# Forgetting attention: the two halves of a block's accumulator, added by GpSimd from a copy and a DMA move instead of by VectorE from PSUM

## The chip, the cores and the metric

The kernel runs on one core of a Trainium2 chip. The metric is the device time of one execution in microseconds (us): 2538.94 us is the median of three runs before the change (2537.07 to 2539.52).

A core has TensorE for matrix products (PE, with PEld for its weight loads), VectorE (DVE), ScalarE (ACT), GpSimd (POOL) and SyncE (SP), which here issues nearly all DMA transfers. PE writes to PSUM, an accumulation memory of banks; the other working memory is SBUF with 128 partitions (rows).

## What is computed

Two layers of an encoder block on 2048 tokens of width 1024, all in float32. Per layer: RMS norm, one input projection, three token mixers, a SiLU gate on each, one output projection, RMS norm and residual. The change touches the third mixer, the forgetting attention with 6 heads of width 64:

```python
cum_f = jnp.cumsum(jax.nn.log_sigmoid(f_logit.astype(jnp.float32)), axis=1)
...
for i in range(s // Q_BLOCK):
    logits = jnp.einsum('bqhd,bkhd->bhqk', qb, kb).astype(jnp.float32) * scale
    logits = logits + cum_f[:, :, q0:q1, None] - cum_f[:, :, None, :q1]
    logits = jnp.where(causal, logits, -jnp.inf)
    p = jax.nn.softmax(logits, axis=-1).astype(v.dtype)
    outs.append(jnp.einsum('bhqk,bkhd->bqhd', p, vb))
...
f_out = f_out.reshape(b, s, F_WIDTH) * jax.nn.silu(f_g)
```

## The kernel before

A float32 product is made of products of a rounded high part and a remainder (H and L). For the attention the values V are stored as 128 columns, 64 of the high part and 64 of the remainder, so one matmul of V with the weights P gives a PSUM tile `acc` of 128 rows: rows 0 to 63 hold P times the high part, rows 64 to 127 P times the remainder. The attention output of a block is the sum of the two halves.

The attention stage of a layer (`fox`) goes over 6 heads h, 4 query blocks s of 512 tokens, and the 4s+4 key tiles j of 128 tokens that block s can see: 40 steps per head, 240 per layer. The instructions of every engine stand in the order in which the program writes them; each engine, and SP's list of DMAs, works its own list in that order and waits where a semaphore says so. A step writes, in this order:

- `l_step`: DVE makes the remainder PL of the last transposed tile (L672);
- `t_step`: PE transposes the softmax weights of a tile three steps ahead of their use (L661), ACT rounds them into PH (L673). For a few tiles (`ON_POOL`) ACT copies the transposed tile out of PSUM (L666) and GpSimd makes PH and PL (L667, L668);
- `e_step`: ACT takes exponentials (L648);
- `s_step`: PE makes scores well ahead (L614, L615), DVE masks them and takes the running minimum (L632);
- `v_step`: PE multiplies V with PH and PL into `acc` (L690, L691); after the last key tile of a block `finish` is added to the background;
- then SP issues one waiting load (`ld.issue()`, L569), and every background generator goes one step on (`bg.tick()`).

`finish` runs once per head and block, 24 times a layer. ACT copies the lower half of `acc` to SBUF (L703), DVE adds the upper half from PSUM into rows 0 to 63 or 64 to 127 of `o2`, by the head's parity e = h % 2 (L705), and sums the softmax denominators (L710). For an even head that is all. For an odd head, with both heads of a pair in `o2`, the reciprocals go through a transpose (L719, L721), a 4 KB DMA store `rd` to device memory (L723), and two DMA loads `gy<-rd` that spread them over the rows (L726); L726 waits until `rd` has landed. GpSimd multiplies them into the gate (L728) and the result into `o2` (L730), and SP stores the block (L732). FX, RA, RB, RC, RD are the steps left between these.

Loads of the next head: at the end of a head's first block, for h > 0, `ld.kv(h + 1)` queues three loads of K and V (512, 512 and 1024 KB, L569), which are issued one per step behind it. For h = 0 and 1 they are issued earlier, in the projection; after head 5 there is none. So they stand in SP's list behind `finish` of block 0 of heads 1 to 4. The tiles named U share 29 buffers.

Of the kernel before, what the change touches and what calls it, by code (L numbers as in the profile page):

```python
# [10 lines left out]
F32 = mybir.dt.float32  # L11
F32R = mybir.dt.float32r
AF = mybir.ActivationFunctionType
ALU = mybir.AluOpType
# [4 lines left out]
P = 128  # L19
# [4 lines left out]
HD = 64  # L24
# [13 lines left out]
FX, RA, RB, RC, RD = 2, 2, 4, 1, 3  # L38
# [32 lines left out]
def wait(n):  # L71
    for _ in range(n):
        yield
# [3 lines left out]
def trunk(ctx, tc, a, out):  # L77
    nc = tc.nc
# [8 lines left out]
    up = ctx.enter_context(tc.tile_pool(name="up", bufs=NU))  # L87
# [3 lines left out]
    def U(name, dt=F32):  # L91
        return up.tile([P, 1024], dt, name=name, tag="u")
# [3 lines left out]
    def bank(name, tag):  # L96
        n, bufs = BANKS[tag]
        return ps.tile([P, n], F32, name=name, tag=tag, bufs=bufs)
# [4 lines left out]
    def small(name, shape, bufs=4):  # L103
        return tp.tile(shape, F32, name=name, tag=name, bufs=bufs)
# [466 lines left out]
    class Fox:  # L571
# [124 lines left out]
        def finish(self, h, s, acc):  # L696
            m, e = divmod(h, 2)
            if e == 0 and s % 2 == 0:
                self.o2[s // 2] = U("o2")
            o2 = self.o2[s // 2][:, (s % 2) * 512:(s % 2 + 1) * 512]  # L700
            yield
            lo = up.tile([HD, 512], F32, name="lo", tag="u")
            nc.scalar.copy(out=lo, in_=acc[HD:P, :])  # L703
            yield
            nc.vector.tensor_tensor(out=o2[e * HD:(e + 1) * HD], in0=acc[0:HD, :], in1=lo, op=ALU.add)  # L705
            if e == 0:
                self.rd[s] = small("rd", [P, 2, 4], bufs=6)
            rd = self.rd[s]
            den = self.den.pop((h, s))
            nc.vector.tensor_reduce(out=rd[:, e], in_=den[:, :, 0:s // 2 + 1], op=ALU.add, axis=AX.X)  # L710
            if e == 0:
                return
            nc.vector.reciprocal(out=rd, in_=rd)
            gy = U("gy")
            g, rb = gy[:, 0:512], gy[:, 512:1024]
            nc.sync.dma_start(out=g, in_=self.gscr[m][:, s * 512:(s + 1) * 512])
            yield from wait(FX)
            T = bank("rT", "S")
            nc.tensor.transpose(T[0:8, 0:P], rd.rearrange("p e r -> p (e r)"), ident)  # L719
            rT = tp.tile([8, P], F32, name="rT", tag="yr")  # L720
            nc.scalar.activation(out=rT, in_=T[0:8, 0:P], func=AF.Copy, scale=0.5)  # L721
            scr = dram.tile([8, P], F32, name=f"rd{self.ld.l}{m}{s}")
            nc.sync.dma_start(out=scr, in_=rT)  # L723
            yield from wait(RA)
            for i in range(2):
                nc.sync.dma_start(out=rb[i * HD:(i + 1) * HD], in_=scr[4 * i:4 * i + 4].rearrange("r p -> (r p)").partition_broadcast(HD))  # L726
            yield from wait(RB)
            nc.gpsimd.tensor_tensor(out=g, in0=g, in1=rb, op=ALU.mult)  # L728
            yield from wait(RC)
            nc.gpsimd.tensor_tensor(out=rb, in0=o2, in1=g, op=ALU.mult)  # L730
            yield from wait(RD)
            nc.sync.dma_start(out=self.y[s][1][m], in_=rb)  # L732
# [204 lines left out]
    for l in range(depth):  # L937
# [3 lines left out]
        for i in fox(fx):  # L941
            if i >= len(fx.V) - OW and i % OD:
                next(og, None)
            if l == depth - 1 and i == len(fx.V) - OPRE:
                op = out_proj(l, y, W, og, x_src, lambda t: out[t * P:(t + 1) * P, :], None, None, None)
            elif i == len(fx.V) - OPRE:
# [5 lines left out]
                op = out_proj(l, y, W, og, x_src, lambda t, x1=x1: x1[t], hT, (nw, W0), cur)  # L952
# [44 lines left out]
```

## Time and profile before

| what | value |
| --- | --- |
| median of three runs | 2538.94 us |
| the profiled execution | 2536.31 us |
| its span in the trace | 2534.5 us |
| PE busy | 2490.1 us, 98% |
| PEld busy | 2141.2 us, 84% |
| DVE busy | 1660.3 us, 66% |
| ACT busy | 1258.1 us, 50% |
| POOL busy | 863.2 us, 34% |
| attention stages (first to last `acc` matmul) | about 795 to 1086 us and 2053 to 2344 us |

The sum in the prediction is made against the profiled execution's 2536.31 us, which lies 2.63 us below the median of the runs; 1.8 us of it lie outside the span. Engine times are sums over the whole span; what an engine does in one stage is read from a view of that stretch. A number in brackets behind a row of an engine is idle time just before it, with what ended it. A row of SPq is a DMA being issued by SP: its start is when SP had waited for everything the DMA waits for, not when the data move.

### The profile page before, as it was taken

How to read it: one execution, taken by the hardware profiler on the slowest of the kernel's cores; microseconds unless marked ns; L12 is line 12 of the kernel's file. 1: busy time of each engine (PE TensorE's matmuls, PEld its weight loads, DVE VectorE, ACT ScalarE, POOL GpSimd, SP SyncE). 2: the span in 40 equal slices, each digit the busy share in tenths (PEclk: the TensorE clock that was granted, in tenths of full speed). 3: DMA queues.
4: the chain of work that ended last, by engine and by line, in shares of the span. 5: the costliest groups of instructions: out<-in, count | busy, mean ns of one | idle time of the engine just before them, and what ended most of it. 6: DMA issues, size and time to landing. Idle time of an engine off the chain costs nothing.

```text
span 2534.5 us, 39560 instructions
## 1 busy us (share of the span) xinstructions
PE 2490.1 (98%) x13112; PEld 2141.2 (84%) x13112; DVE 1660.3 (66%) x4161; ACT 1258.1 (50%) x2967; POOL 863.2 (34%) x1384
## 2 busy tenths in 40 slices
PE   9999999999999999999999999999999999999998
PEld 8988899787888888878898889997878888887887
DVE  5544477666668999844454445776666789998433
ACT  7634434333335888843344444333333368888222
POOL 3111367444433334331120114664443333244200
PEclk9999999999999999999999999999999999999999
DMA  6435411101041345253432354111010414543443
GB/s 210 120 92 122 110 46 34 41 14 42 10 110 41 102 110 147 72 182 132 138 124 75 98 121 114 29 38 44 13 39 18 106 42 108 122 135 105 154 149 117
DMA packets 187061, 229.87 MB, mean 91 GB/s; under 512 B 23272, under 2 KB 128680, under 8 KB 185320
## 3 DMA queue, kind: packets, MB, share of 16 engines
q1 hardware_dynamic: 186712, 227.08, 32.0%
q8 instruction: 104, 1.70, 0.3%
q14 instruction: 101, 0.83, 0.1%
q10 hardware_dynamic: 144, 0.26, 0.0%
HBM read 149.20 MB, written 78.09 MB: 90 GB/s over the span
## 4 chain that ended last, share of the span: by engine, by line
PE 83%; DVE 9%; ACT 3%; POOL 2%; issue 2%; DMA 1%; SPq 0%; ACTq 0%; POOLq 0%; DVEq 0%
PE oo L870 13%; PE z L491 10%; PE z L493 10%; PE z L492 10%; PE T L661 6%; PE z L267 5%; PE z L266 5%; PE z L268 5%; PE S L614 4%; PE S L615 4%; PE acc L691 3%; PE acc L690 3%; DVE HL L178 3%; ACT HL L176 2%; PE sc L371 1%
## 5 line engine op out<-in xcount | busy, mean ns | idle before, releaser
L491 PE MATMUL z<-HL 128*128 128x512 f32 (+2 forms) x1536 | 589.4, 384 | 2.3 <-ACT HL L176 2.3
L493 PE MATMUL z<-HL 128*128 128x512 f32 (+2 forms) x1536 | 560.8, 365 | 1.2 <-DVE HL L178 1.0
L492 PE MATMUL z<-HL 128*128 128x512 f32 (+2 forms) x1536 | 559.4, 364 | 0.6 <-POOL HL L178 0.6
L178 DVE TENSOR_TENSOR HL<-hT,HL 128x512 fp32r<-128x512 f32 x576 | 425.3, 787 | 42.0 <-ACT HL L176 33.6
L870 PE MATMUL oo<-HL 128*128 128x512 f32 x1488 | 355.4, 395 | 0.1
L178 POOL TENSOR_TENSOR HL<-wf,HL 128x384 fp32r<-128x384 f32 (+2 forms) x162 | 190.1, 1179 | 431.4 <-ACT HL L176 277.5
L176 ACT CAST HL<-hT 128x512 fp32r<-128x512 f32 x576 | 323.6, 625 | 0.0
L870 PEld LDWEIGHTS oo<-HL 128*128 128x128 f32 x1488 | 273.3, 188 | 57.8 <-DVE HL L178 0.5
L493 PEld LDWEIGHTS z<-HL 128*128 128x128 f32 x1536 | 289.0, 188 | 36.1 <-DVE HL L178 2.6
L491 PEld LDWEIGHTS z<-HL 128*128 128x128 f32 x1536 | 289.7, 189 | 25.3 <-ACT HL L176 3.2
L492 PEld LDWEIGHTS z<-HL 128*128 128x128 f32 x1536 | 290.5, 189 | 22.8 <-POOL HL L178 0.9
L672 DVE TENSOR_TENSOR PHL<-T,PHL 128x512 fp32r<-128x512 f32 (+3 forms) x402 | 241.1, 603 | 16.3 <-ACT PHL L673 16.2
L673 ACT CAST PHL<-T 128x512 fp32r<-128x512 f32 (+3 forms) x402 | 206.2, 520 | 57.2 <-PE T L661 41.0
L266 PE MATMUL z<-HL 128*128 128x512 f32 x576 | 224.5, 390 | 0.0
L268 PE MATMUL z<-HL 128*128 128x512 f32 x576 | 224.1, 389 | 0.0
L267 PE MATMUL z<-HL 128*128 128x512 f32 x576 | 224.1, 389 | 0.0
L350 ACT COPY v<-z 128x128 f32<-128x128 f32 x96 | 25.5, 266 | 382.4 <-DVE w L346 382.3
L614 PE MATMUL S<-kv,q 128*128 128x512 f32 (+1 forms) x480 | 210.9, 441 | 3.0 <-DVE mn L632 3.0
L690 PE MATMUL acc<-PHL,kv 128*128 128x512 f32 x480 | 181.0, 377 | 0.0
L691 PE MATMUL acc<-PHL,kv 128*128 128x512 f32 x480 | 176.3, 367 | 1.3 <-POOL PHL L668 0.7
L648 ACT ACTIVATE row<-row,mn 128x1024 f32<-128x1024 f32 (+2 forms) x192 | 158.2, 824 | 35.5 <-DVE mn L632 35.5
L615 PE MATMUL S<-kL,q 66*128 66x512 f32 (+1 forms) x480 | 175.8, 366 | 0.0
(160 smaller groups left out, 4343.7 us busy)
## 6 DMA issues: line engine op xcount, KB each, us to landing
x<-x SPq DMA_DIRECT2D x48, 512.0 KB
qk<-zHL SPq DMA_DIRECT2D x192, 128.0 KB
wf<-w_in SPq DMA_DIRECT2D x96, 192.0 KB
vscr<-vv SPq DMA_DIRECT2D x32, 384.0 KB
wf<-w_in SPq DMA_DIRECT2D x48, 256.0 KB
kv<-qk SPq DMA_DIRECT2D x24, 512.0 KB
kv<-vscr SPq DMA_DIRECT2D x12, 1024.0 KB
q<-qk SPq DMA_DIRECT2D x48, 256.0 KB
```

What stands on the lines that cost most here:

```text
L176: nc.scalar.copy(out=v(H), in_=src)
L178: eng.tensor_tensor(out=v(L), in0=src, in1=v(H), op=ALU.subtract)
L266: mm(z, lhsT=wH[:, c], rhs=H, start=(k == 0), stop=False)
L267: mm(z, lhsT=wH[:, c], rhs=L, start=False, stop=False)
L268: mm(z, lhsT=wL[:, c], rhs=H, start=False, stop=(k == KT - 1))
L491: mm(z[:, :n], lhsT=H[:, c], rhs=wH[:, :n], start=(k == 0), stop=False)
L492: mm(z[:, :n], lhsT=H[:, c], rhs=wL[:, :n], start=False, stop=False)
L493: mm(z[:, :n], lhsT=L[:, c], rhs=wH[:, :n], start=False, stop=(k == KT - 1))
L614: mm(S[:, :n], lhsT=Q[0][:, qc], rhs=K[:, kc], start=True, stop=False)
L615: mm(S[:, :n], lhsT=Q[1][0:HD + 2, qc], rhs=self.ld.C[h][c // 2][0:HD + 2, (c % 2) * 512:(c % 2) * 512 + n], start=False, stop=True)
L690: mm(self.acc[:, c0:], lhsT=V[:, j], rhs=PH[:, c0:], start=(j == 0), stop=False)
L870: mm(oo[g], lhsT=x[:, c], rhs=w[g][i], start=(k == 0 and first), stop=(k == KT - 1 and last))
```

## The change

ACT now copies all 128 rows of `acc` into the left half of a 1024-wide tile `two`. A DMA on SP's list moves the other head half's 64 rows beside the 64 rows that belong to this head. GpSimd adds the two, 8 steps later for an even head and just ahead of the gate product for an odd one. DVE's add is gone. The line numbers of what follows move by 3 or 4: L719, L723, L726, L728, L730, L732 become L722, L726, L729, L732, L734, L736.

```diff
             yield
-            lo = up.tile([HD, 512], F32, name="lo", tag="u")
-            nc.scalar.copy(out=lo, in_=acc[HD:P, :])
+            two = U("two")
+            mine, other = (slice(e * HD, (e + 1) * HD), slice((1 - e) * HD, (2 - e) * HD))
+            nc.scalar.copy(out=two[:, 0:512], in_=acc)
+            nc.sync.dma_start(out=two[mine, 512:1024], in_=two[other, 0:512])
             yield
-            nc.vector.tensor_tensor(out=o2[e * HD:(e + 1) * HD], in0=acc[0:HD, :], in1=lo, op=ALU.add)
...
             if e == 0:
+                yield from wait(FX + RA + RB)
+                nc.gpsimd.tensor_tensor(out=o2[mine], in0=two[mine, 0:512], in1=two[mine, 512:1024], op=ALU.add)
                 return
...
             yield from wait(RB)
+            nc.gpsimd.tensor_tensor(out=o2[mine], in0=two[mine, 0:512], in1=two[mine, 512:1024], op=ALU.add)
             nc.gpsimd.tensor_tensor(out=g, in0=g, in1=rb, op=ALU.mult)
```

SP's list before, around block 0 of head 1 in layer 0: the last loads of queries, the three loads of head 2's K and V (`kv_9310`), the gate, then the store `rd` and the two loads that wait for it.

```order
L569 DMA q_9269<-qk001_238 128x512
L569 DMA q_9269<-qk001_238 66x512
L569 DMA kv_9310<-qk011_241 64x2048
L716 DMA gy_9326<-gscr00_244 128x512
L569 DMA kv_9310<-qk011_241 64x2048
L569 DMA kv_9310<-vscr0_243 128x16x128
L723 DMA rd000_9366<-rT_9364 8x128
L726 DMA gy_9326<-rd000_9366 64x512 x2
```

SP's list after, at the same place; `two_9243` is the move of head 0, block 3, and `two_9311` that of head 1, block 0.

```order
L705 DMA two_9243<-two_9243 64x512
L569 DMA q_9272<-qk001_238 128x512
L569 DMA q_9272<-qk001_238 66x512
L705 DMA two_9311<-two_9311 64x512
L569 DMA kv_9314<-qk011_241 64x2048
L719 DMA gy_9329<-gscr00_244 128x512
L569 DMA kv_9314<-qk011_241 64x2048
L569 DMA kv_9314<-vscr0_243 128x16x128
L726 DMA rd000_9369<-rT_9367 8x128
L729 DMA gy_9329<-rd000_9369 64x512 x2
```

Each move waits for ACT's copy of its block; what stands below it in SP's list now comes after that copy, the loads of K and V of the next head among it.

GpSimd's list before, from the tile of head 1, block 1 (128x384) to that of block 2, key tile 4 (`PHL_9476`):

```order
L667 TENSOR_SCALAR PHL_9349<-Ts_9350 128x384
L668 TENSOR_TENSOR PHL_9349<-Ts_9350,PHL_9349 128x384
L728 TENSOR_TENSOR gy_9326<-gy_9326 128x512
L667 TENSOR_SCALAR PHL_9476<-Ts_9477 128x512
L668 TENSOR_TENSOR PHL_9476<-Ts_9477,PHL_9476 128x512
L730 TENSOR_TENSOR gy_9326<-o2_8595,gy_9326 128x512
```

GpSimd's list after, at the same place; L714 adds head 0's block 3, L731 head 1's block 0:

```order
L667 TENSOR_SCALAR PHL_9352<-Ts_9353 128x384
L668 TENSOR_TENSOR PHL_9352<-Ts_9353,PHL_9352 128x384
L714 TENSOR_TENSOR o2_8968<-two_9243 64x512
L731 TENSOR_TENSOR o2_8595<-two_9311 64x512
L732 TENSOR_TENSOR gy_9329<-gy_9329 128x512
L667 TENSOR_SCALAR PHL_9481<-Ts_9482 128x512
L668 TENSOR_TENSOR PHL_9481<-Ts_9482,PHL_9481 128x512
L734 TENSOR_TENSOR gy_9329<-o2_8595,gy_9329 128x512
```

The two adds stand ahead of the gate product; the gate product stands ahead of the next tile for PE, as it did.

## Rows read from the trace of the kernel before

**Rows 1.** Attention stages: length, busy PE, PEld, DVE, ACT, POOL; clock, DMA share, GB/s.

```profile
795.00:1092.00 297.00, 290.61 (x1781) 245.15 (x1780) 266.23 (x723) 254.60 (x559) 110.91 (x119) 1.00 0.42 114
2052.00:2349.00 297.00, 290.26 (x1776) 244.79 (x1776) 267.17 (x724) 254.91 (x559) 110.48 (x119) 1.00 0.41 112
```

**Rows 2.** Waits of PE, whole span: total us, times, longest.

```profile
PE T L661 <- DVE PHL L672: 7.2, 15, 1.3
PE S L614 <- DVE mn L632: 3.0, 7, 0.9
PE acc L691 <- POOL PHL L668: 0.7, 1, 0.7
```

**Rows 3.** Groups by line and shape: xcount, busy us, mean ns, idle before.

```profile
L673 ACT CAST PHL<-T 128x512 fp32r<-128x512 f32 x282 | 162.2, 585 | 31.1 <-PE T L661 22.4 <-PE S L614 5.8 <-POOL w L348 0.7
L705 DVE TENSOR_TENSOR o<-acc,lo 64x512 f32<-64x512 f32 x48 | 32.7, 681 | 0.8
L730 POOL TENSOR_TENSOR gy<-o,gy 128x512 f32<-128x512 f32 x24 | 30.9, 1287 | 0.9
L703 ACT COPY lo<-acc 64x512 f32<-64x512 f32 x48 | 28.0, 583 | 1.2
```

**Rows 4.** Timeline of SP's issues, head 1's block 0: start us, us, what.

```profile
846.41 0.75 SPq L569 DMA_DIRECT2D q<-qk  x2
847.21 0.45 SPq L569 DMA_DIRECT2D kv<-qk  x1
...
849.76 0.59 SPq L569 DMA_DIRECT2D kv<-vscr  x1
856.35 1.14 SPq L723 DMA_DIRECT2D rd<-rT  x1
861.47 1.09 SPq L726 DMA_DIRECT2D gy<-rd  x2
```

**Rows 5.** Two stretches: length, mean granted clock, DMA share, GB/s.

```profile
847.00:860.00 13.00, 1.00 0.99 212
860.00:862.00 2.00, 1.00 0.06 15
```

**Rows 6.** SP's own waits: total us, times, longest.

```profile
SPq L726 <- DMA rd<-rT: 29.0, 18, 4.5
```

**Rows 7.** DMA issues of the whole program: count, KB of each.

```profile
q<-qk SPq DMA_DIRECT2D x48, 256.0 KB
q<-qk SPq DMA_DIRECT2D x48, 132.0 KB
```

**Rows 8.** Timeline of ACT, the copy of head 1's block 0.

```profile
853.44 0.58 ACT L703 COPY lo<-acc 64x512 f32<-64x512 f32 x1
```

**Rows 9.** Timeline of POOL behind the gate product of head 1's block 0.

```profile
865.46 1.29 POOL L728 TENSOR_TENSOR gy<-gy 128x512 f32<-128x512 f32 x1 [7.96 <-DMA gy<-rd]
866.71 0.63 POOL L667 TENSOR_SCALAR PHL<-Ts 128x512 fp32r<-128x512 f32 x1
867.42 1.29 POOL L668 TENSOR_TENSOR PHL<-Ts,PHL 128x512 fp32r<-128x512 f32 x1
```

**Rows 10.** Timeline of PE at the tile that POOL makes there.

```profile
868.76 0.50 PE L691 MATMUL acc<-PHL,kv 128*128 128x512 f32 x1
```

**Rows 11.** The same gate product in the three other places of its kind.

```profile
962.23 1.29 POOL L728 TENSOR_TENSOR gy<-gy 128x512 f32<-128x512 f32 x1 [7.25 <-DMA gy<-rd]
...
2123.63 1.28 POOL L728 TENSOR_TENSOR gy<-gy 128x512 f32<-128x512 f32 x1 [8.63 <-DMA gy<-rd]
...
2220.27 1.29 POOL L728 TENSOR_TENSOR gy<-gy 128x512 f32<-128x512 f32 x1 [7.40 <-DMA gy<-rd]
```

**Rows 12.** SP's issues at the start of head 2, where `rd` precedes the loads.

```profile
902.09 0.29 SPq L723 DMA_DIRECT2D rd<-rT  x1
902.42 0.45 SPq L569 DMA_DIRECT2D kv<-qk  x1
903.31 1.09 SPq L726 DMA_DIRECT2D gy<-rd  x2
```

**Rows 13.** POOL's next tile for PE in head 2, block 2.

```profile
914.65 0.62 POOL L667 TENSOR_SCALAR PHL<-Ts 128x512 fp32r<-128x512 f32 x1 [2.04 <-ACT Ts L666]
```

**Rows 14.** Early stretches: length, PE busy (x), clock, DMA share, GB/s.

```profile
6.00:14.00 8.00, 4.43 (x21) 1.00 0.98 301
14.00:18.00 4.00, 3.81 (x16) 0.57 0.79 258
```

## The prediction, made before the changed kernel ran

> **What bounds the kernel now.** I read the busy times of the two attention stages first, then the waits of PE, then the durations of the instructions that go or come, and last, step by step, what SP and GpSimd issue around one block. The first view [rows 1] gives PE 290.6 of 297 us and 290.3 of 297: PE is the bound of the stage, with some 6.5 us of idle time in each. The same rows have DVE at 266 of 297, which is 90%, ACT at 255 and POOL at 111. The waits of PE [rows 2] say who ends the idle time: DVE's remainder of a transposed tile 7.2 us over the whole span, DVE's score minimum 3.0, GpSimd's tiles 0.7. So everything that the removal of a DVE instruction can give back of the waits seen is 10.2 us, in both layers together, and only where an L705 lies just ahead. GpSimd, which gets the work, is far from busy, but its tiles feed PE directly, and it works in order.
>
> **The change part by part.** The sum is made against the profiled execution, 2536.31 us; the median of the runs is 2.63 us above it, and I add that at the end.
>
> *DVE's add.* 48 of 681 ns go [rows 3], 32.7 us of an engine that PE waits on for 10.2 us. Nothing of the 32.7 is on PE's own path, so the gain lies between 0 and 10.2 us. The wait goes only where DVE had no other idle time between the add and the tile PE waits for, and the add is in 24 of 240 steps of a layer. I take 4, somewhat under half, and keep 0 to 10.
>
> *ACT's copy.* It grows from 64 to 128 rows. L703 with 64 rows took 583 ns, L673 with 128 rows and the same 512 columns 585 [rows 3]. The cost is 0.
>
> *GpSimd's adds.* 48 of 64x512, both inputs in SBUF. The nearest row is L730, 128x512 with both inputs in SBUF, 1.287 us [rows 3]; DVE's and ACT's rows do not shrink with 64 rows, so I take 1.29 and 62 us in all, 31 a layer, on an engine with 297 − 111 = 186 us of idle time there [rows 1]. Where one stands right ahead of a tile for PE it could cost up to 1.29 us. In the odd heads it stands where POOL waits for the loads `gy<-rd` anyway, 7.96 us in head 1 [rows 9], and disappears in that wait. At the start of head 2 the next tile has 2.04 us of idle time in front [rows 13], which the 1.29 fit into. I take 0, and keep up to 3 us (four such places, in heads 2 and 4 of both layers, at 0.8 each).
>
> *The move on SP's list.* This is the term that decides. The move waits for ACT's copy, and SP goes no further before that. Queued behind it at head 1, block 0, are the loads of head 2's K and V, the gate, the store `rd` and the two loads `gy<-rd` of the odd head's denominators; GpSimd waits for the last, and PE for GpSimd.
>
> Before, SP ran ahead of the other engines: it issued the first load of K at 847.21 [rows 4], though ACT's copy of the block in front of it in the program ran only from 853.44 to 854.02 [rows 8]. The DMA engines were then full until 860 (share 0.99 from 847 to 860, 0.06 after) [rows 5]. `rd`, 4 KB, was issued at 856.35 into that, and SP could issue the loads that wait for it only at 861.47 [rows 4], when the big loads had drained. Where `rd` goes ahead of them, in head 2, the same step took 1.22 us (902.09 to 903.31) [rows 12]. SP's waits for `rd` agree: 29.0 us over 18 times, the longest 4.5 [rows 6]. So a small transfer stands behind the big ones, and what counts is when these start.
>
> After, the first load of K comes when the copy is done and the move is issued: 854.02 + 0.45 (an issue of the length of the first load's [rows 4]) = 854.47, 7.26 us later than 847.21. Two things are then different ahead of `rd` in the DMA queue. The two query loads, 256 + 132 KB [rows 7], were issued just before the loads of K and are now out of the way 4 us earlier; a move of 64 rows x 512 x 4 bytes = 128 KB is new. That is 260 KB less, at 212 GB/s 1.25 us. So the loads `gy<-rd` come 7.26 − 1.25 = 6.0 us later, at 867.5, and the gate product at 865.46 + 6.0 = 871.5.
>
> GpSimd has no slack there. In its list the gate product stands in front of L667 and L668, the tile for PE's next product, which ran without a pause behind it [rows 9] and ended at 868.71; PE's L691 began at 868.76 [rows 10]. Of the 6.0 us PE waits 6.0 − 0.05. The three other places of this kind, head 3 of layer 0 and heads 1 and 3 of layer 1, have the same waits of POOL for `gy<-rd`, 7.25, 8.63 and 7.40 us [rows 11], and the same order in SP's list. Heads 2 and 4 have the big loads behind `rd` already; there the move comes 0.8 us ahead of `gy<-rd`, which the slack of 2.04 takes. Head 5 has no loads behind it. So 4 places at 6.0 − 0.05 are 23.8; I take 23, since the other three may have a little more slack. The ends: 7.26 a place if the 260 KB do not help (29 us), and 0 if `rd` does not wait in line.
>
> *PE's clock behind these waits.* The granted clock is 1.00 in both stages [rows 1], which is 2.4 GHz. Early in the program PE was busy 4.43 of 8 us, and the mean clock of the next 4 us was 0.57, most of it at the lower level of 1.2 GHz [rows 14]: 4 x 0.43 = 1.7 us lost. A wait of nearly 6 us leaves PE idler than that, so I take 1.7 at each of the four places, 6.8 us, and keep 0 as the other end. The Trainium skill (TensorE: Matmul & The Clock Gate, "What's actually happening") states that an engine without activity is put back to half the clock and has to be busy for a while to get it back. By that rule the sum stands with this term; by the attention stages' rows alone, which never leave 1.00, it is 6.8 less; those rows hold no wait as long as the new one.
>
> The sum: 2536.31 − 4 + 0 + 0 + 23 + 6.8 = 2562.1 us, and 2.63 more against the median: 2565 us.
>
> **The rivals.**
>
> *No new wait.* The move is there, but `gy<-rd` lands in time, because the small store does not wait for the loads ahead of it, or because SP issues the loads early after all. For it speaks that in head 2 a load of K, issued between `rd` and `gy<-rd`, holds up neither issue [rows 12]. The Trainium skill (DMA: Bandwidth & Descriptors, "Queues, rings and completion order") states that completion is not in order per issuing engine, so a small DMA may be done ahead of a larger one. Against it speaks the store that was issued at 856.35 and let SP go on only at 861.47, after the drain at 860 [rows 4, 5]. By that rule the four waits would be 0; the trace here stands against it. The time: 2538.9 − 4 + up to 3, 2535 to 2538 us, no change that can be told.
>
> *DVE is what PE really waits for.* With DVE at 90% the 10.2 us of waits go nearly all, and waits too short to be seen as idle time of PE with them, while the loads land in time: 2538.9 − 10 = 2529 us, faster. It decides if more is saved on DVE than the four places cost, that is if these stay under about 2.5 us each. For it speaks only DVE's load; against it that 4 x 6 is more than twice all the waits of PE on DVE.
>
> *The stall without the clock.* The four waits come, and PE keeps its full clock: 2565 − 6.8 = 2558 us. For it speaks the 1.00 of the stages; against it the 0.57 [rows 14].
>
> **How the numbers follow.** The measurement tells about 0.2%, 5 us, from no change. My forecast with the clock falling: 0.55, 2565 us; the stall without the fall: 0.30, 2558; no new wait: 0.10; faster: 0.05. The first two are slower than 2544, so slower 0.85, same 0.10, faster 0.05. The forecast's own ends: 2538.9 + 4 x 5.4 − 10 = 2550 at the low end without the clock (5.4 if the move of 128 KB costs nothing), and 2538.9 + 29 + 6.8 + 3 = 2578 at the high end with no gain. Taking 2547 to 2577 leaves out the two cases on the other side, 0.15, and a little above.
>
> **What the profile after would show.** In head 1, block 0 of layer 0: the first load of K issued right behind the move, about 854.5 if nothing before it moved; `gy<-rd` near 867.5; the gate product L732 near 871.5 with POOL waiting for `gy<-rd` before it, for longer than 7.96 us less the two adds in front; PE's waits on GpSimd's tiles up from 0.7 to some 20 us over at least 4 times, about 6 the longest; a granted clock under 1.00 in the 4 us behind each. In head 5, and in the projection, nothing of that. DVE's busy time down by 33 us, POOL's up by 62, an add at 1.29 us, ACT's copy at 0.58, and PE's waits on DVE down from 10.2 to about 6. I am wrong if SP issues the loads of K before the copy, if `rd` lands within 2 us of its issue while they run, or if PE's wait at those four tiles stays under 1 us.

## The result, and the profile after

| | before | after |
|---|---|---|
| time, median of 4 runs each | 2539.05 us | 2571.65 us (2571.28 to 2574.10) |
| span of the profiled execution | 2534.5 us | 2569.4 us |
| mean granted clock | 0.999 | 0.992 |

The changed kernel is slower: ratio 1.0131, 95% interval 1.0118 to 1.0143. Forecast were 2565 us in a range of 2547 to 2577.

The busy times of the two attention stages, which are now 315 us long (297 in [rows 1]); columns: length, busy us (count) of PE, PEld, DVE, ACT and POOL, granted clock, DMA share, GB/s:

```profile
795.00:1110.00 315.00, 296.42 (x1788) 250.86 (x1789) 255.38 (x700) 252.45 (x562) 139.90 (x142) 0.97 0.44 119
2070.00:2385.00 315.00, 295.49 (x1781) 250.24 (x1780) 254.42 (x698) 251.03 (x558) 139.98 (x142) 0.97 0.43 116
```

VectorE does less, GpSimd more, PE is idle 19 us in each stage and the granted clock is no longer 1.00. The waits of PE (total us, times, longest) name the place; before it was 0.7 us on GpSimd's tiles [rows 2]:

```profile
PE acc L690 <- POOL PHL L667: 20.1, 4, 5.4
...
PE T L661 <- DVE PHL L672: 9.9, 9, 2.7
PE acc L691 <- DVE PHL L672: 2.8, 2, 1.4
...
PE acc L691 <- POOL PHL L668: 2.2, 4, 0.6
PE S L614 <- DVE mn L632: 1.9, 2, 0.9
```

Four waits of about 5 us on the tile that GpSimd makes in L667. SP's list around head 1, block 0, answers to [rows 4]:

```profile
849.63 0.47 SPq L705 DMA_DIRECT2D two<-two  x1
850.20 0.96 SPq L569 DMA_DIRECT2D q<-qk  x2
853.61 0.47 SPq L705 DMA_DIRECT2D two<-two  x1
854.13 0.59 SPq L569 DMA_DIRECT2D kv<-qk  x1
...
856.59 5.91 SPq L726 DMA_DIRECT2D rd<-rT  x1
866.91 1.10 SPq L729 DMA_DIRECT2D gy<-rd  x2
```

The loads of Q and those of K and V each wait behind a move, the store `rd` is issued while they run (its issue alone takes 5.91 us), and the denominators' loads are issued at 866.91, not 861.47. What follows on GpSimd, and then on PE:

```profile
870.64 1.26 POOL L732 TENSOR_TENSOR gy<-gy 128x512 f32<-128x512 f32 x1 [10.83 <-DMA gy<-rd]
```

```profile
872.54 0.80 PE L690 MATMUL acc<-PHL,kv 128*128 128x512 f32 x1 [4.99 <-POOL PHL L667]
873.89 0.80 PE L691 MATMUL acc<-PHL,kv 128*128 128x512 f32 x1 [0.56 <-POOL PHL L668]
```

```profile
870.00:874.00 4.00, 0.90 (x2) 0.39 (x2) 0.00 (x0) 0.00 (x0) 3.28 (x4) 0.66 0.69 192
874.00:878.00 4.00, 4.00 (x13) 3.33 (x14) 0.76 (x2) 0.60 (x2) 2.69 (x3) 0.50 0.43 122
```

Before, the same matmul took 0.40 us. Here it takes 0.80: behind the wait the granted clock is 0.50, the lower level of 1.2 GHz (the windows' columns are those above).

To say where the 34.9 us of span went I compared the starts of PE's 480 matmuls L690 (240 steps in each layer) of the two traces, step by step. The four places (heads 1 and 3, seven steps from the waiting one, block 2, key tile 4, in each layer) cost 8.1, 7.3, 8.6 and 8.2 us: 32.2. All other steps up to head 5's last block gain 7.5. From head 5's last block to the end of what follows it, the kernel loses 9.8 in the two layers together, and 0.4 lies ahead of the attention stages: 32.2 − 7.5 + 9.8 + 0.4 = 34.9. The same three numbers ("places", "other steps", "tail") are given for the experiments below; they are of one execution each, which lies up to 3.1 us from the median.

The tail was not in the forecast. In head 5 the output weights `wf` are loaded and converted beside the last steps. SP's list around the first steps of the last block, before and in the changed kernel:

```profile
1069.98 0.33 SPq L732 DMA_DIRECT2D yT<-gy  x1
1070.41 1.13 SPq L716 DMA_DIRECT2D gy<-gscr  x1
1071.59 0.42 SPq L769 DMA_DIRECT2D wf<-w_out  x1
```

```profile
1083.87 0.48 SPq L705 DMA_DIRECT2D two<-two  x1
1084.52 0.46 SPq L736 DMA_DIRECT2D yT<-gy  x1
1085.03 0.44 SPq L719 DMA_DIRECT2D gy<-gscr  x1
1085.57 0.39 SPq L773 DMA_DIRECT2D wf<-w_out  x1
```

The first L690 of that block starts at 1070.59 and at 1083.05. Counted from there, the weights now stand behind a move and are issued at 2.52 us and not at 1.00, and land at 8.2 and not at 5.6. ScalarE waits for them, 0.28 us before and 3.13 now, and behind its cast stand the casts that VectorE and PE need:

```profile
1076.23 0.62 ACT L176 CAST HL<-wf 128x512 fp32r<-128x512 f32 x1 [0.28 <-DMA wf<-w_out]
```

```profile
1091.39 0.62 ACT L176 CAST HL<-wf 128x512 fp32r<-128x512 f32 x1 [3.13 <-DMA wf<-w_out]
```

```profile
1093.27 1.12 PE L661 MATMUL T<-ident,rows 128*128 128x128 f32 x4 [2.44 <-DVE PHL L672]
```

### The profile page after: what moved, and what is told of

The parts are those of the page before. It is cut to its first block, busy times and chain, and to the rows that moved or that the text cites. A ratio compares the mean times of both kernels' runs of the same rounds, so it can differ in the third digit from the quotient of the medians.

```text
span 2569.4 us, 39805 instructions
## 1 busy us (share of the span) xinstructions
PE 2498.7 (97%) x13112; PEld 2150.4 (84%) x13112; DVE 1637.9 (64%) x4113; ACT 1252.2 (49%) x2967; POOL 927.9 (36%) x1432
## 5 line engine op out<-in xcount | busy, mean ns | idle before, releaser
L178 DVE TENSOR_TENSOR HL<-hT,HL 128x512 fp32r<-128x512 f32 x576 | 425.7, 789 | 42.1 <-ACT HL L176 33.6
L690 PE MATMUL acc<-PHL,kv 128*128 128x512 f32 x480 | 184.9, 385 | 20.1 <-POOL PHL L667 20.1
L691 PE MATMUL acc<-PHL,kv 128*128 128x512 f32 x480 | 180.2, 375 | 5.6 <-DVE PHL L672 2.8
```

Source lines behind the costliest of these rows:

```text
L178: eng.tensor_tensor(out=v(L), in0=src, in1=v(H), op=ALU.subtract)
```

## The experiments

Theory: the move stands in SP's in-order list, waits for ScalarE's copy, and so starts what is queued behind it late. Rival A: GpSimd's 62 us of adds stand ahead of its tiles for PE. Rival B: the moves' 128 KB each crowd the loads. All times are medians, the ratios against before's runs beside them.

| run | expected by the theory | measured | ratio, 95% | places | other steps | tail |
|---|---|---|---|---|---|---|
| e1_move_on_act | 2531–2537 | 2550.93 | 1.0029–1.0054 | 7.3 | 1.1 | 6.1 |
| e3_move_alone | 2581 | 2578.23 | 1.0138–1.0164 | 33.5 | 0.0 | 8.9 |
| e4_no_move | 2531–2542 | 2549.42 | 1.0025–1.0049 | 0.1 | 5.8 | 6.3 |
| e5_kv_ahead | 2540 | 2600.17 | 1.0227–1.0254 | 25.4 | 30.7 | 7.4 |
| e6_two_blocks_back | 2536–2543 | 2543.27 | 1.0005–1.0023 | 0.0 | −3.2 | 9.6 |
| e7_one_block_back | 2556–2566 | 2571.52 | 1.0112–1.0142 | 31.4 | −3.2 | 10.1 |
| e8_wide_copy | 2531 or 2539 | 2538.33 | 0.9989–1.0006 | 1.0 | 0.2 | 0.3 |
| e9_no_dve_add | 2539 or 2531 | 2533.09 | 0.9964–0.9985 | 2.4 | −6.7 | 3.1 |
| e10_clock_kept | 2559–2564 | 2569.66 | 1.0097–1.0126 | 33.6 | −6.9 | 7.5 |
| e11_tail_back | 2533 | 2534.36 | 0.9975–0.9993 | 0.0 | −3.3 | 1.3 |
| e12_only_block_0 | 2534.6 | 2537.17 | 0.9982–0.9999 | −0.2 | −1.4 | 2.2 |
| e13_clock_kept_2 | 2560–2565 | 2564.57 | 1.0075–1.0109 | 25.1 | −6.2 | 9.1 |

### The move alone, and the change without it

```diff
-lo = up.tile([HD, 512], F32, name="lo", tag="u")
+two = U("two")
+lo = two[0:HD, 0:512]
 nc.scalar.copy(out=lo, in_=acc[HD:P, :])
+nc.sync.dma_start(out=two[HD:P, 512:1024], in_=lo)
```

> The kernel before, with VectorE's add from PSUM kept and no add on GpSimd; added is only a move of 128 KB behind ScalarE's copy on SP's list, whose result nobody uses. Theory (SP's list): the four waits and the loss around the end of head 5 come as in the changed kernel, without the relief of VectorE: 2539 + 32 + 10 = 2581 us. Rival A (GpSimd's adds): 2539 us. Rival B (the bytes): about 2581 us.

2578.23 us. Nothing but the move was added to the kernel before, and the four places cost 33.5 us (7.8 to 8.9 each). Rival A is out for them. The mirror image takes the move out of the changed kernel:

```diff
-nc.scalar.copy(out=two[:, 0:512], in_=acc)
-nc.sync.dma_start(out=two[mine, 512:1024], in_=two[other, 0:512])
+nc.scalar.copy(out=two[mine, 0:512], in_=acc[mine, :])
+nc.scalar.copy(out=two[mine, 512:1024], in_=acc[other, :])
```

> The changed kernel without the move: ScalarE copies the own half and the other half by two copies of 64 rows straight to where GpSimd's add reads them. GpSimd's adds stay, ScalarE has 48 copies of 0.58 us more. Theory (SP's list): 2531 to 2542 us, the relief of VectorE less what 28 us more on ScalarE cost. Rival A (GpSimd's adds): about 2570 us. Rival B (the bytes): as the theory.

The places are gone (0.1 us), with all of GpSimd's adds in place. But the time is 2549.42, 7 us above the range: the relief did not come. ScalarE's second copy, for which the range left up to 11 us, is on PE's path. VectorE's tile at the same step, first in the changed kernel, then without the move:

```profile
853.13 0.69 DVE L672 TENSOR_TENSOR PHL<-T,PHL 128x512 fp32r<-128x512 f32 x1 [0.32 <-ACT PHL L673]
```

```profile
853.74 0.69 DVE L672 TENSOR_TENSOR PHL<-T,PHL 128x512 fp32r<-128x512 f32 x1 [0.50 <-ACT PHL L673]
```

0.6 us later, which is the length of the second copy (0.58), and VectorE has longer to wait for ScalarE. Relieving VectorE by work for ScalarE gives nothing here: 28 us more on ScalarE turned −7.5 into +5.8.

### The move on another queue

```diff
-nc.sync.dma_start(out=two[mine, 512:1024], in_=two[other, 0:512])
+nc.scalar.dma_start(out=two[mine, 512:1024], in_=two[other, 0:512])
```

> The changed kernel, but the move of the half is issued from ScalarE's own queue, right behind ScalarE's copy, and not from SP's list. Bytes, GpSimd's adds and ScalarE's copy stay. Theory (the move stands in SP's in-order list and holds what is behind it until the copy is done): the four waits of PE on GpSimd's tile of 5 us and more are gone, and the 10 us lost around the end of head 5 too; what is left is the relief of VectorE, so 2531 to 2537 us. Rival A (GpSimd's adds stand ahead of its tiles for PE): nothing changes, about 2570 us. Rival B (the bytes of the moves, 128 KB each, crowd the loads): nothing changes, about 2570 us.

2550.93 us, between the theory and the rivals, and outside its range. SP issues the K loads at 847.20 again, and the waits of 5 us are gone. Two things eat the rest. Each issue stops ScalarE for half a microsecond, in the same place as the second copy above:

```profile
849.12 0.58 ACT L704 COPY two<-acc 128x512 f32<-128x512 f32 x1
849.73 0.47 ACTq L705 DMA_DIRECT2D two<-two  x1
850.24 0.27 ACT L666 COPY Ts<-T 128x128 f32<-128x128 f32 x1 [0.54 <-PE S L615]
```

And the move now runs beside the big loads: issued at 849.73, it landed only at 858.8. SP's longest wait between 844 and 868 us:

```profile
SPq L726 <- DMA two<-two: 8.4, 1, 8.4
```

The store `rd` is issued at 858.82, 2.5 us later than before. It does not read the move's data, but in the trace this move and the store count on one semaphore (number 102), and SP waits on it for the move to land before it issues the store. In head 3 the waits this leaves are 1.29 and 0.85 us, and that place still costs 4.3. The Trainium skill (DMA: Bandwidth & Descriptors, "Issuing engines are not separate DMA queues") states that transfers issued by different engines run on the same 16 DMA engines and interleave, so that another issuer saves no more than the issue. The trace agrees that they share the engines: the move took 9 us to land beside the loads. Here another issuer saved more than the issue, though: with the move's wait for ScalarE out of SP's list the places cost 7.3 us and not 32.2. All 48 moves with their bytes are still there, so rival B does not explain the 32.2.

### The loads ahead of the move

```diff
-if s == 0 and j == 3 and h > 0:
+if s == 0 and j == 0 and h > 0:
     ld.kv(h + 1)
```

> The changed kernel with the loads of the next head's K and V queued three steps earlier, so that they stand ahead of the move of head 1's (and 3's) block 0 in SP's list; move, bytes and GpSimd's adds stay. Theory (SP's list, and the small store behind the big loads): the four places' 32 us go, the 10 us around the end of head 5 and the relief of VectorE stay: about 2540 us. Rival A (GpSimd's adds): about 2570 us. Rival B (the bytes): about 2570 us. If the move alone, and not the loads behind it, makes the denominators late, 2555 us and more.

A clear miss: 2600.17 us. SP's list at head 1, and further down at head 2:

```profile
849.51 1.19 SPq L569 DMA_DIRECT2D kv<-qk  x2
...
851.43 5.58 SPq L569 DMA_DIRECT2D q<-qk  x2
...
903.68 1.09 SPq L569 DMA_DIRECT2D kv<-qk  x2
...
917.74 1.09 SPq L729 DMA_DIRECT2D gy<-rd  x2
```

The loads passed one move but not the move of the block before (848.95), so they start 2.3 us later than in the kernel before; `gy<-rd` comes 2.3 us later too (863.74 against 861.47). The two q loads behind them took 5.58 us to issue, and the next move (857.13) and the store came after all of it. In head 2, where the store was ahead of the K loads [rows 12], it is now behind them (912.69): `gy<-rd` is issued at 917.74, and GpSimd waits 10.30 us for the denominators. Heads 1 and 3 lose 5.4 to 7.3 us each, heads 2 and 4, which lost next to nothing, now 9.8 to 9.9. So my reading of the list was wrong, but the run speaks for the mechanism from another side: what decides is which big loads stand ahead of the small store, and when they start. A run with only the store moved ahead of the loads was not made.

### The way of before in a few blocks

```diff
+old = (s, h) in ((0, 1), (0, 3), (3, 0), (3, 2))
+if old:
+    lo = two[0:HD, 0:512]
+    nc.scalar.copy(out=lo, in_=acc[HD:P, :])
+    yield
+    nc.vector.tensor_tensor(out=o2[mine], in0=acc[0:HD, :], in1=lo, op=ALU.add)
+else:
...
```

> The changed kernel, with the way of before (64-row copy, VectorE's add, no move) put back in 8 of the 48 blocks only: block 3 of heads 0 and 2 and block 0 of heads 1 and 3, in both layers, so that no move stands between the q loads and the K and V loads of the four places. Theory (SP's list): the four waits go, 32 us; the relief and the loss around the end of head 5 stay: 2540 us, 2536 to 2543. Rival A (GpSimd's adds, 40 of 48 stay): about 2567 us or more. Rival B (bytes; 40 of 48 moves stay, those close to the four places go): no number of its own.

2543.27 us: with 40 of 48 moves and adds still there, the places cost 0.0. It is the eight blocks around them. This run takes their adds and bytes away too; that it is the moves, for where they stand, follows with the move alone (rival A) and the move on ScalarE's queue (rival B). With only half of these blocks in the way of before (`old = s == 0 and h in (1, 3)`):

> The same with 4 blocks only, block 0 of heads 1 and 3 in both layers: the move of the block before (issued at 849.63 in the changed kernel) still stands ahead of the q, K and V loads, so that they start 3.8 us later than before (850.20 against 846.41) and not 7. Theory (SP's list, the store rd drains behind the loads): the denominators' loads 3.8 us later than in before and not 5.4, PE's wait at the four places 3.3 us and not 5.0, the total 2556 to 2566 us. Rival (it is the move next to the K loads that counts, for its bytes or its wait): the waits go, 2540 us.

2571.52 us, outside the expectation: the rival is out, and the theory's price is too low. SP's issues at head 1, then head 3:

```profile
850.75 0.47 SPq L569 DMA_DIRECT2D kv<-qk  x1
...
864.82 1.69 SPq L737 DMA_DIRECT2D gy<-rd  x2
...
955.13 0.47 SPq L569 DMA_DIRECT2D kv<-qk  x1
...
970.42 1.09 SPq L737 DMA_DIRECT2D gy<-rd  x2
```

In head 1 the loads and the denominators come about as much earlier as expected, and PE's wait is 3.49 us (expected 3.3; 4.99 in the changed kernel; in layer 1 4.00 and 5.36). In head 3 it is 4.58 and 5.39 us, no less than with both moves (4.50, 5.23): there the loads start earlier too, but it takes 15.3 us from the first K load to `gy<-rd` (before: 14.0; in head 1 14.1, before 14.3). Why they drain more slowly in head 3 stays open. And a shorter wait did not save its share: behind 3.49 us the clock still fell, and the place cost 7.5 us where it had cost 8.1.

### What is the relief?

```diff
-nc.scalar.copy(out=lo, in_=acc[HD:P, :])
+nc.scalar.copy(out=two[:, 0:512], in_=acc)
...
-nc.vector.tensor_tensor(out=o2[e * HD:(e + 1) * HD], in0=acc[0:HD, :], in1=lo, op=ALU.add)
+nc.vector.tensor_tensor(out=o2[e * HD:(e + 1) * HD], in0=acc[0:HD, :], in1=two[HD:P, 0:512], op=ALU.add)
```

> The kernel before with one thing of the change: ScalarE copies all 128 rows of the accumulator and not 64; VectorE's add stays and reads rows 64 to 127 of the copy; no move, no add on GpSimd. Theory C (the relief of 0.3 to 0.6 us at some steps comes from ScalarE, whose 128-row copy holds it 0.46 us and the 64-row copy 0.61): 2531 us, the steps at block 1 of each head 0.3 to 0.6 us earlier. Theory D (the relief comes from VectorE's missing add): 2539 us.

2538.33 us, no change: the wide copy alone gives nothing. The other half of the pair:

```diff
-nc.scalar.copy(out=lo, in_=acc[HD:P, :])
+nc.scalar.copy(out=o2[e * HD:(e + 1) * HD], in_=acc[HD:P, :])
...
-nc.vector.tensor_tensor(out=o2[e * HD:(e + 1) * HD], in0=acc[0:HD, :], in1=lo, op=ALU.add)
```

> The kernel before without VectorE's add: ScalarE copies rows 64 to 127 straight to the output tile, 64 rows as before, and the other half of the accumulator is left out of the sum. No move, no add on GpSimd. Theory C (the relief is ScalarE's): 2539 us. Theory D (the relief is VectorE's): 2531 us.

2533.09 us, 0.25% faster than before. The relief is VectorE's in the main, theory D: 6.7 us in the other steps, against 7.5 in the changed kernel. It lies in the first four steps of block 1 of each head, 6.4 us here and 8.5 in the changed kernel. The 2.1 us more are all in the odd heads; the wide copy may give them once VectorE's add is gone, which was not tested.

GpSimd's adds are nearly free in the body of the stage, but not quite. In heads 2 and 4 the steps from block 2, key tile 4 to 8 lose 1.0 us together in the changed kernel and up to 2.8 in the others with most moves on SP's list and most adds (one block back), but 0.2 or less with the move alone and with the adds and no move.

Then the way of the changed kernel only where a step had come earlier behind it (`old = not (s == 0 and h in (0, 2, 4, 5))`):

> The way of the changed kernel in block 0 of heads 0, 2, 4 and 5 only (8 of 48 blocks), the others as before. The steps that came earlier without VectorE's add (0.54, 0.36, 0.37, and 0.31 + 0.55 us, each layer) all follow such a block 0. Theory (only there VectorE's add is on PE's path, and GpSimd's adds elsewhere cost a little): 2539 - 4.3 = 2534.6 us. Rival (all the missing adds together make the relief): 2538 us.

2537.17 us, between the two. The steps in heads 0 and 5 came earlier, those in heads 2 and 4 did not (the four steps of 0.36 us are missing). For heads 1 and 3 the runs above say which blocks count: they gain 0.81 us each in the changed kernel, 0.21 with their block 0 as before, and nothing with block 3 of the head ahead as before too. In this run the block 3 ahead of heads 2 and 4 was as before; that it is the one missing was not tried.

### The clock

```diff
+if (s, j) == (2, 4) and h in (1, 3):
+    for _ in range(13):
+        mm(self.acc, lhsT=V[:, j], rhs=zz, start=False, stop=False)
 mm(self.acc[:, c0:], lhsT=V[:, j], rhs=PH[:, c0:], start=(j == 0), stop=False)
```

> The changed kernel with work for PE in the four waits: 13 matmuls of 128x512 that add zeros to the accumulator stand directly ahead of the matmul that waits for GpSimd's tile (heads 1 and 3, block 2, j = 4, both layers). A matmul of that form takes 0.396 us at the full clock, so 13 take 5.1 us, about the waits of 4.5 to 5.4. Theory (the 2 to 3 us that each place loses beyond its wait are the half clock): the granted clock stays at 1.00 behind the four places, the matmuls behind take 0.396 and not up to 0.795 us, and 4 times 2 to 3 us come back: 2559 to 2564 us. Rival (they are the pipeline's own restart, ScalarE's and VectorE's tiles late after the wait): nothing comes back, 2570 to 2574 us.

2569.66 us, inconclusive: the filling (`zz` is a tile of zeros) was too short.

```profile
866.83 3.19 PE L695 MATMUL acc<-zz,kv 128*128 128x512 f32 x13
872.16 0.49 PE L696 MATMUL acc<-PHL,kv 128*128 128x512 f32 x1 [2.14 <-POOL PHL L670]
```

Thirteen matmuls took 3.19 us, not 13 x 0.396 = 5.1. A matmul's duration in the profile overlaps the next one's; the time it takes in a row of them is the distance between starts. 2.14 and 0.85 us of wait were left, and the granted clock behind them was 0.57. One of the four executions took 2561.49 us at a mean granted clock of 0.997, the other three 2569.6 to 2570.3 us at 0.994, which speaks for the theory. So again, with 22 ahead of the waiting matmul and 4 behind it:

> The same test of the clock with the waits really filled. In the run before it the 13 matmuls followed one another every 0.245 us (3.19 us for 13), since each begins before the one ahead has ended, and left 1.9 to 2.5 us of the wait open, with a granted clock of 0.57 behind it. Here 22 stand ahead of the matmul that waits (22 x 0.245 = 5.4 us) and 4 between it and the next one (0.85 us of wait there). Theory (the 2 to 3 us behind each wait are the half clock): the granted clock stays at 1.00, the matmuls behind take 0.396 us again, 4 times 2 to 3 us come back, less up to 0.5 each where the filling is longer than the wait: 2560 to 2565 us. Rival (restart of the pipeline): 2570 to 2574 us.

2564.57 us, inside the range, 7.1 us less than the changed kernel:

```profile
866.85 5.30 PE L695 MATMUL acc<-zz,kv 128*128 128x512 f32 x22
...
873.38 0.60 PE L664 MATMUL T<-ident,row 128*128 128x128 f32 x4
```

```profile
870.00:874.00 4.00, 4.00 (x21) 3.27 (x20) 0.00 (x0) 0.00 (x0) 3.92 (x4) 1.00 0.55 156
874.00:878.00 4.00, 4.00 (x24) 3.38 (x24) 3.02 (x11) 2.58 (x6) 3.25 (x4) 1.00 0.57 166
```

The clock stays at 1.00 behind all four places, the four transposes take 0.60 us and not 1.05, and the four places cost 25.1 us and not 32.2. The work added changes no value: it only keeps PE busy while it waits.

### The tail

> The 8 blocks of before as in the run of two blocks back, and the way of before in blocks 1 to 3 of head 5 too: 14 of 48 blocks as before, 34 with the move and GpSimd's add. Theory (around the end of head 5 the move and the add hold the loads of the output weights, which ScalarE's casts wait for, 5 us a layer): 2543 - 10 = 2533 us. Rival (that loss has nothing to do with head 5's own blocks): 2543 us.

The edit is `old` as above with `or (h == 5 and s > 0)`. 2534.36 us, 8.9 less than without it and 1.4 from the expectation: the tail belongs to head 5's own blocks. SP's list there has no move, as in the kernel before, and the weights that ScalarE waited for go out at 1071.22 (before 1071.59):

```profile
1071.22 0.42 SPq L782 DMA_DIRECT2D wf<-w_out  x1
```

It is the move, and not GpSimd's add. The step of key tile 7 in head 5's last block loses 2.4 to 3.4 us a layer in all seven kernels with SP's moves in blocks 1 to 3 of that head (2.8 and 3.4 with the move alone, 3.0 and 3.1 in the changed kernel) and at most 0.5 in the other six; the kernel with the adds and no move loses 1.6 and 3.1 us in that block, but at other steps. The rest of the tail was not taken apart: without any move, single executions still differ there by up to 3.1 us. This version, with 34 blocks in the new way and 14 in the old, is faster than both kernels: ratio 0.9984 to before, interval 0.9975 to 0.9993.

## Why the prediction was right, and where it was not

*The move on SP's list.* Right, in place and in size. The first load of K came at 854.13 (forecast 854.5), `gy<-rd` at 866.91 (867.5), the gate product at 870.64 (871.5), PE's waits were 20.1 + 2.2 us over four places (about 20, four times), the longest 5.4 (about 6), and began one matmul earlier than forecast, at L690. With the clock held up the places cost 25.1 us; the sum had 23. The rival "no new wait" falls with the store: the Trainium skill (DMA: Bandwidth & Descriptors, "Queues, rings and completion order") states that completion is not in order, but here the loads that wait for the store were issued 10.3 us after its issue began, and in all four places 0.1 to 0.3 us after the last big load had landed. In the kernel before, one of the four came 0.9 us ahead of that landing.

*PE's clock.* Right: 6.8 forecast, 7.1 measured by the filling. The rival "stall without the clock" (2558 us) is out.

*DVE's add.* The sign was right, 4 us was too little: 6.7 without the add, 7.5 in the changed kernel, within the 0 to 10.2. PE's waits on VectorE over the whole span did not fall to 6, though: they are 14.6 (9.9 + 2.8 + 1.9). Ahead of head 5's last blocks they fell from 5.6 to 2.8, from there on they rose from 5.3 to 11.7. VectorE's busy time fell by 22 us and not 33, and by 23 where only the adds are missing, so 48 x 681 ns was too much as well; in part because listed times overlap (from an add's start to the next instruction's it took 0.62 us on average).

*ACT's copy and GpSimd's adds.* Both were taken as 0. The wide copy alone changes the time by 0.03%, with an interval of −0.11 to +0.06%. The adds, together with the moves, cost 1.0 us in heads 2 and 4, where up to 3 had been kept. POOL's busy time rose by 65 us (62 forecast).

*Head 5.* This is the step that failed: "Head 5 has no loads behind it", and of the waits "In head 5, and in the projection, nothing of that". There are loads behind it, the output weights: they stand behind the move in SP's list, and ScalarE, which waited 0.28 us for them, waits 3.13. The tail cost 9.8 us, 6.1 of them at the steps of key tile 7 in the two layers; the sum had nothing for it. Put right, the sum is 2565 + 9.8 for the tail, + 2.4 for the places (32.2, not 29.8), − 3.5 for VectorE (7.5, not 4) = 2573.7, against 2571.65; the profiled executions differ by 34.9 us of span, the medians by 32.6. That the time still came out inside the range is in part luck: the missing tail and the relief that was priced too low pull in opposite directions.

## What to carry to other kernels

Before a transfer is added to an in-order list, write down everything that stands behind it until the next small transfer that some engine waits for, to the end of the kernel and not only where the pattern repeats; here 8 of 48 moves cost 32 us, those of head 5's last blocks about 9 in the two layers together, and the others next to nothing. Price a new wait of PE with what follows it: here waits of 4.5 to 5.4 us cost 7.3 to 8.6 with the fall of the clock, and one of 3.49 us still 7.5. Work taken from one engine is only a gain if what it is given to has no place on the path: GpSimd's adds were nearly free, half a microsecond more on ScalarE was not.

## What the runs showed of the hardware that was not expected

- *A copy of fewer rows held ScalarE longer.* With 64 rows from the upper half to the lower, the instruction behind started 0.61 us after it in 46 of 48 cases; with 128 rows in place, 0.47 us in 46 of 48. Both are listed with 0.58 us. It need not be the way between the halves: in the run without the move, copies of 64 rows in place held the next one for 0.58 us as well. The kernel before, then the one with the wide copy:

```profile
849.25 0.58 ACT L703 COPY lo<-acc 64x512 f32<-64x512 f32 x1
849.86 0.27 ACT L666 COPY Ts<-T 128x128 f32<-128x128 f32 x1
```

```profile
849.05 0.58 ACT L703 COPY two<-acc 128x512 f32<-128x512 f32 x1
849.52 0.28 ACT L666 COPY Ts<-T 128x128 f32<-128x128 f32 x1
```

- *An issue can itself take microseconds.* The store `rd` took 5.3 to 6.2 us to issue at the four places of the changed kernel, and two pairs of q loads 5.58 and 6.75 us where K and V stood ahead of them; before, the store took 0.26 to 1.75 us. The kernel before has such issues too: the `kL` load behind K and V in heads 2 and 4, 4.67 to 6.02 us.
- *The clock fell after short waits too.* In the run with the move on ScalarE's queue, behind waits of 1.29 and 0.85 us, with PE busy 2.12 of the 4 us around them, the granted clock of the next 4 us was 0.72.
- *A row of 128x512 matmuls of this kernel's type steps at 0.23 us at the full clock,* each listed with 0.39 to 0.40 (22 took 5.30 us; without the last one's 0.39, 4.91 / 21). The Trainium skill (TensorE: Matmul & The Clock Gate, "Step-by-step: what each phase is for") states that one matmul's drain overlaps the next one's fill and gives 216 ns between starts at 512 columns; the trace agrees in kind, and is some 8% above the figure.
